# Moving 23 on-chip swaps to ScalarE's DMA queue, some evacuations and roundings to VectorE, in a new order of all instructions

## The chip, the cores and the metric
The kernel runs on one core of one Trainium2 chip. The metric is device time in microseconds from launch to end. The core has TensorE (PE; its weight loads are the row PEld), VectorE (DVE), ScalarE (ACT), GpSimd (POOL) and SyncE (SP), which here only issues DMAs. "q" behind an engine's name is its sequencer, which waits and issues.

## The reference
Two layers (DEPTH 2) over 256 tokens of width 1024, all in float32. Each layer:

```python
n = rmsnorm(h, norm_g[i])
z = n @ w_in[i] + b_in[i]
(c_val, c_glu, c_gate, p_in, p_gate, q, k, v, a_gate, qi, ki, wi) = jnp.split(z, cut, axis=-1)
ya = conv_module(c_val, c_glu, ...) * jax.nn.silu(c_gate)      # depthwise conv of 31 taps, layernorm, 256x256
yb = pool_mixer(p_in, ...) * jax.nn.silu(p_gate)               # causal means over 2, 4, 8, 16 tokens
q, k, qi, ki = rope(q), rope(k), rope(qi), rope(ki)            # rotary: x1*cos - x2*sin, x2*cos + x1*sin
yc = sparse_attention(q, k, v, qi, ki, wi) * jax.nn.silu(a_gate)
h = h + jnp.concatenate([ya, yb, yc], axis=-1) @ w_out[i]
h = h + (p[i] @ ple_w[i]) * jax.nn.sigmoid(h @ ple_gate_w[i])
```

The attention has 8 heads of 64. An indexer (4 heads of 64) scores all keys of a query, the 64 best causal keys take part in the softmax, the others don't. A final rmsnorm closes the trunk.

## The kernel before, in words
Activations lie transposed: 128 features per partition block, 256 tokens along the row. A float32 product is made from three products of rounded parts: each operand is split into `hi` (rounded to TensorE's float32r form) and `lo` (the remainder, also in that form), and hi*hi, hi*lo and lo*hi are summed in a PSUM bank (`mm3`). One such 128x128 block against 256 tokens is three matmuls of 256 columns (line 208, tile `bank`), and the program bundles six of them.

Weights come as chunks of 2048 columns (1024 KB) into a ring of three `raw` tiles by one DMA each on SP's queue (line 294, `dma`). Each chunk has two halves of 1024 columns. A half is rounded to `hi` by a copy (line 242 on ScalarE, 244 on VectorE), and `lo` is raw minus hi (`sub_hi`, line 262 on VectorE, 264 on POOL). `hi` and `lo` have rings of six tiles. A new load has to wait until both halves of the chunk that lay in its `raw` tile have been split.

The input projection is worked chunk by chunk (`gemm_in`, 8 bundles each). Chunk numbers are in the tags: 5 and 6 are Q0 and Q1 (the two halves of q), 7 and 8 are K0 and K1, 9 and 10 are V0 and V1, 13 is QI (the indexer's queries), 3 the pooling input, 2, 4, 11, 12 gates. After a chunk VectorE multiplies the bank with the token's rms factor (line 252, `bank<-bank,rb`), and `evac` adds the bias on ScalarE (line 217).

For a rotary chunk (`rope_pair`) the two evacuations write `z`. Since the rotation mixes partitions 32 apart, four SBUF-to-SBUF DMAs of 64 KB copy quarters of `z` to `zs` with the halves swapped; these are "the swaps". For the indexer key (`e ki`) there are ten of 32 or 64 KB. With five rotary chunks (Q0, Q1, K0, K1, QI) of four swaps and one of ten, a layer has 30 swaps, the kernel 60, all on SP's queue. Then `rope` makes dst = z*cos, zs = zs*sin and dst = dst+zs (lines 252 on VectorE, 254 on POOL); dst is `zrq` for q, `zrk` for k, `qir` for the indexer. `z` and `zs` are rings of two tiles, so a chunk's evacuation waits for the rotation of the chunk two before it.

In the trace the rows `zrk<-z,f` and `zrq<-z,f` are cosine products, `zs<-zs,f` sine products, `zrk<-zrk,zs` and `zrq<-zrq,zs` the adds.

Layer 0's order after that: the indexer scores (4 matmuls each for two blocks of queries, then a relu on ScalarE and weighted sums `sc` on VectorE), the search for the 64 best (8 rounds of MAX8 and MATCH_REPLACE8 on VectorE, lines 651 and 653) which ends in the penalty `pen` (line 275), then attention logits (qk), whose first use on VectorE (line 693, `lg<-bank,pen`) adds the penalty, the exponentials (line 217), transposes (line 212) and the product with v. In between VectorE works through 62 taps of the convolution (line 269, `bank<-f,f,bank`).

What engine does what, and in which order, is not left to a scheduler: `Order.add` collects 1726 operations, each with its possible "ways" (an engine with a cost estimate), and `Order.issue` emits them in the order of the string `ORDER`, two characters for each operation. The number they encode is 3 * operation + way. `PORT` adds a few more waits between operations by number. Within an engine the instructions run in the order in which they are emitted; an instruction that waits holds all behind it on its engine.

```python
i, way = divmod(len(DIGITS) * DIGITS.index(ORDER[2 * k]) + DIGITS.index(ORDER[2 * k + 1]), 3)
assert i not in made and all(d in made for d in self.ops[i][1])
made[i] = self.ops[i][0][way][4]()
```

The end of the kernel (`last_gate`) works with tokens on partitions: gate product, sigmoid, residual, sums of squares, the final scaling and five output DMAs, of which two were already on ScalarE's queue.

Of the kernel before, what the change touches and what calls it, by code (L numbers as in the profile page):

```python
# [87 lines left out]
    "Q3M-TNM1S7KaTQN<S=Q6TTN?Q9TLMgTWNBQ<NEM?Q?MBMEMHN&QBMKN-MNQEN3MjS@V<N9MQQHNHMTMmMpSBMsNKMvSvSEMyQKSISyNNSKTZUQ"
    "QNSONTNWS|NQU$T^NdNgNjNZT#NmNpMWMZS:M^NsMaMdN^T&U+NvNbTaNyQQV?TdQTM|N|O#QWVCSQV|QZSTOHQ^OKO&O*U-O.VEU0QdUUQaON"
    "OQTgOTOWO0OZO3O6O9O<O?OBOEQgQjQmQpU3QsTjU6QvS^QySZU9Q|O^TmW#R#U<TpR&U?TsW(R*R0TvUBR-T*UEVaT-UHR3R6UKR9R<VQVHR?"  # L90
    "VKRBRET0V#XERHUWV&RKRNU[RQVTT3VNRTVyV*VdT6V^VgV-T9VjWaW*VvT<VmW6W.W9U^UaUdZ<UgUjWdUmWhUpUsW0UvWEW3UyWNU|WHV0WB"
    "V3WQV6W^WKWjV9VWVZVpWmXHWZVsWpXNXLZdW<WsYWX*W?WvZ?X&XBWTZBWWX-WyXQX0X3XTX?[0W|X6X#XaZgXWX9Y#ZEZjXyXZX|ZHX<X^Xd"
    "Y*Xg[EXmY-XpY&ZmY0XsXvYEXjZqYHZKY3ZWYNY<ZNY?ZTY6YZ[3Y^YyY9YaY|ZQYKYBYd[HZ#ZZZvYQ[K[9Z^[&Yg[6Zs[<ZaZy[NZ|[Q[*[#"
    "YT[m[?[B[TZ&[W[p[ZZ*[s[^Z-[v[a]?[y[d]B[|]E]#[-[j[g]&]^]*]H]-]0]a]K]dZ0]N]gZ3]jZ6YjYmZ9Yp]mYsYv]p]9]|]Q^#]v]<^&"
    "]T]4^*]X]6]Z^-]s^0^3]y^9^6^<^?^C^N^I^E^Q^K"
# [3 lines left out]
    61: 129, 153: 323, 176: 157, 635: 267, 869: 937, 926: 922, 986: 1027, 987: 988, 992: 878, 1112: 1156,  # L99
    1130: 1129, 1488: 1500, 1684: 1682,  # L100
# [11 lines left out]
class Order:  # L112
# [200 lines left out]
def trunk(ctx: ExitStack, tc: tile.TileContext, xT, pT, w_in, w_ki, w_v, w_out, w_gate, w_ple,  # L313
# [54 lines left out]
    def chunk(tag, src, width=2048, pieces=1, late=VECTOR_LATE):  # L368
# [7 lines left out]
        for a in range(0, width, width // 2):  # L376
# [108 lines left out]
    def layer(l, sqs, ple):  # L485
# [7 lines left out]
        for k in range(0, KT, 2):  # L493
# [4 lines left out]
            R.copy(nhi[:, k:k + 2, :], n, "act dve" if l == 0 else "act")  # L498
# [33 lines left out]
        def evac(dst, pb, c, func):  # L532
            for j in range(2):
                R.act(dst[j], pb[:, j * S:(j + 1) * S], func, bias=bias(c, j))
# [72 lines left out]
        R.act(z[:, 0, :], pt[:, :S], AF.Identity, bias=col(l, SP_B + 28))  # L607
# [23 lines left out]
        for t in (1, 0):  # L631
# [8 lines left out]
            for e in range(2):  # L640
                R.act(pbs[e][:, :2 * nk], pbs[e][:, :2 * nk], AF.Relu, scale=0.125)
# [30 lines left out]
        for t in (1, 0):  # L672
# [3 lines left out]
            for g0 in range(0, 4, nh):  # L676
# [27 lines left out]
                for i in range(nh):  # L704
# [10 lines left out]
                   rinv[:, t, :].rearrange("p (e f) -> p f e", e=2).unsqueeze(3).to_broadcast([128, 4, 2, 64]), "act")  # L715
# [3 lines left out]
            R.copy(wide, on, "act")  # L719
# [31 lines left out]
        for t in range(2):  # L751
            R.act(cn[:, t, :], pc[:, t * 256:(t + 1) * 256], AF.Identity, bias=nm[:, t:t + 1], scale=rl[:, t:t + 1])
# [13 lines left out]
        for j in range(2):  # L766
            R.act(pwb[:, j, :], pw_[:, j * S:(j + 1) * S], AF.Identity, bias=col(l, SP_PWB + j))
# [273 lines left out]
```

## Time and profile before

| what | us |
|---|---|
| median of 3 runs | 340.71 (338.14 to 340.8) |
| the profiled execution, its own time | 336.73 |
| its span, first to last instruction | 334.9 |
| PE busy | 316.4 |
| DVE busy | 243.9 |
| ACT busy | 192.3 |
| POOL busy | 160.7 |

The profiled execution is a single one, 1.2% below the median of the timed runs. Busy times count instructions on the engine's data path, not its waits or DMA issues; matmuls overlap, so that each lasts about 0.28 us in the rows while they start about 0.118 us apart. A row of a timeline is: start, length, engine, line, operation, out<-in, shapes, count, and in brackets how long the engine stood idle before it and what ended that.

### The profile page before, as it was taken

Reading aid. Unit: us, or ns where it says so; the run is one execution under the profiler, and the core shown is the slowest. Engines: PE = TensorE matmul, PEld = TensorE weight load, DVE = VectorE, ACT = ScalarE, POOL = GpSimd, SP = SyncE. Lnnn points to the kernel's source line nnn. Section 1 sums busy time; section 2 is a strip of 40 time slices with the busy share of each in tenths; the row PEclk is TensorE's granted clock in tenths of the full one; section 3 lists DMA queues with packets and bytes.
Section 4 is the critical chain, followed back from the end, with each engine's and each line's share of the span. In section 5 each row is a group of like instructions: output and inputs, shape, how many; then the busy total and the mean of one; then the engine's idle time right before and its main releaser. Section 6 shows DMA issues by size and latency. Waiting matters only on the chain.

```text
span 334.9 us, 6450 instructions
## 1 busy us (share of the span) xinstructions
PE 316.4 (94%) x2468; PEld 295.6 (88%) x2469; DVE 243.9 (73%) x549; ACT 192.3 (57%) x337; POOL 160.7 (48%) x112
## 2 busy tenths in 40 slices
PE   7899999895999999999999999999999999999990
PEld 3789999894889999999999999999888999998870
DVE  3977999895798553758798587998895862558374
ACT  3668434614768863547498544545657583637452
POOL 1004566958986583000112464997978665302011
PEclk9999999997999999999999999999999999999996
DMA  7988675382060309364616747536433327262003
GB/s 211 342 288 324 218 281 191 96 243 95 12 250 2 127 22 387 126 252 137 242 32 238 293 157 278 183 103 240 150 127 125 127 93 283 99 227 119 0 1 126
DMA packets 13551, 57.32 MB, mean 171 GB/s; under 512 B 2128, under 2 KB 3280, under 8 KB 8016
## 3 DMA queue, kind: packets, MB, share of 16 engines
q1 hardware_dynamic: 13232, 56.52, 48.2%
q8 instruction: 19, 0.31, 0.4%
q10 hardware_dynamic: 288, 0.39, 0.3%
q14 instruction: 12, 0.10, 0.1%
HBM read 52.45 MB, written 1.05 MB: 160 GB/s over the span
## 4 chain that ended last, share of the span: by engine, by line
PE 76%; DMA 8%; POOL 4%; SPq 4%; issue 3%; ACT 2%; DVE 1%; POOLq 0%; DVEq 0%
PE bank L208 73%; DMA raw<-in_w_in_dram 5%; SPq L294 4%; DMA zs<-z 4%; PE bank L212 3%; POOL zs L254 1%; POOL qir L254 1%; ACT hi L242 1%; POOL zrk L254 1%; POOL ag L254 0%; POOL zrq L254 0%; DVE zrk L252 0%; POOL acc L254 0%; ACT vt L242 0%; ACT bank L217 0%
## 5 line engine op out<-in xcount | busy, mean ns | idle before, releaser
L208 PE MATMUL bank<-xhi,hi 128*128 128x256 f32 x464 | 133.0, 289 | 0.2 <-ACT ple L242 0.2
L242 ACT ACTIVATE hi<-raw 128x1024 fp32r<-128x1024 f32 (+2 forms) x95 | 94.5, 1015 | 64.8 <-DMA raw<-in_w_in_dram 25.7
L208 PE MATMUL bank<-xlo,hi 128*128 128x256 f32 (+1 forms) x464 | 130.3, 282 | 0.9 <-DVE xlo L262 0.9
L208 PE MATMUL bank<-xhi,lo 128*128 128x256 f32 x448 | 126.3, 282 | 0.3 <-POOL lo L264 0.3
L264 POOL TENSOR_TENSOR lo<-raw,hi 128x1024 fp32r<-128x1024 f32 (+2 forms) x43 | 102.6, 2398 | 46.9 <-ACT hi L242 46.8
L208 PEld LDWEIGHTS bank<-xhi,hi 128*128 128x128 f32 x464 | 87.8, 190 | 2.4 <-issue 1.0
L208 PEld LDWEIGHTS bank<-xlo,hi 128*128 128x128 f32 (+1 forms) x464 | 87.2, 188 | 1.7 <-DVE xlo L262 1.4
L208 PEld LDWEIGHTS bank<-xhi,lo 128*128 128x128 f32 x448 | 85.1, 190 | 0.5 <-POOL lo L264 0.5
L262 DVE TENSOR_TENSOR lo<-raw,hi 128x1024 fp32r<-128x1024 f32 (+2 forms) x55 | 60.1, 1122 | 16.8 <-ACT hi L242 12.9
L269 DVE SCALAR_TENSOR_TENSOR bank<-f,f,bank 128x256 f32<-128x256 f32 x116 | 56.1, 483 | 1.6
L208 PE MATMUL bank<-yhi,hi 128*128 128x256 f32 x128 | 36.6, 286 | 0.0
L208 PE MATMUL bank<-ylo,hi 128*128 128x256 f32 x128 | 36.0, 281 | 0.0
L208 PE MATMUL bank<-yhi,lo 128*128 128x256 f32 x128 | 35.9, 281 | 0.0
L208 PE MATMUL bank<-hi,xhi 128*128 128x256 f32 (+2 forms) x100 | 32.1, 321 | 0.8 <-DVE vt L252 0.8
L208 PE MATMUL bank<-lo,xhi 128*128 128x256 f32 (+2 forms) x100 | 31.3, 313 | 0.0
L208 PE MATMUL bank<-hi,xlo 128*128 128x256 f32 (+2 forms) x100 | 31.2, 312 | 0.0
L252 DVE TENSOR_TENSOR bank<-bank,rb 128x512 f32<-128x512 f32 (+1 forms) x26 | 17.2, 674 | 15.0 <-PE bank L208 14.8
L208 PEld LDWEIGHTS bank<-ylo,hi 128*128 128x128 f32 x128 | 24.1, 188 | 0.3 <-DVE ylo L262 0.3
L208 PEld LDWEIGHTS bank<-yhi,hi 128*128 128x128 f32 x128 | 24.1, 188 | 0.2
L208 PEld LDWEIGHTS bank<-yhi,lo 128*128 128x128 f32 x128 | 24.1, 188 | 0.0
L208 PEld LDWEIGHTS bank<-hi,xhi 128*128 128x128 f32 x100 | 18.8, 188 | 2.7 <-DVE vt L252 1.0
L208 PEld LDWEIGHTS bank<-hi,xlo 128*128 128x128 f32 x100 | 18.9, 188 | 1.3
(165 smaller groups left out, 457.3 us busy)
## 6 DMA issues: line engine op xcount, KB each, us to landing
raw<-in_w_in_dram SPq DMA_DIRECT2D x25, 1024.0 KB, 5.7
raw<-in_w_out_dram SPq DMA_DIRECT2D x8, 1024.0 KB, 4.9
raw<-in_w_gate_dram SPq DMA_DIRECT2D x8, 1024.0 KB, 5.2
zs<-z SPq DMA_DIRECT2D x40, 64.0 KB, 2.3
raw<-in_w_v_dram SPq DMA_DIRECT2D x2, 1040.0 KB, 5.9
raw<-in_w_ple_dram SPq DMA_DIRECT2D x8, 256.0 KB, 4.6
f<-in_xT_dram SPq DMA_DIRECT2D x4, 256.0 KB, 6.5
raw<-in_w_in_dram SPq DMA_DIRECT2D x4, 256.0 KB, 6.0
```

Source lines behind the costliest of these rows:

```text
L208: lambda: self.nc.tensor.matmul(o, lhsT, rhs, start=start, stop=stop, skip_group_check=True))],
L212: self.add([("pe", 195, 109, None, lambda: self.nc.tensor.transpose(o, i, ident))], [i, ident], [o], sort=2)
L242: ways.append(self.on_act(o, i, lambda: self.nc.scalar.activation(o, i, AF.Copy)))
L252: ways.append(self.on_dve(n, lambda: self.nc.vector.tensor_tensor(o, a, b, op), late=late))
L254: ways.append(self.on_pool(n, lambda: self.nc.gpsimd.tensor_tensor(o, a, b, op)))
L262: ways.append(self.on_dve(n, lambda: self.nc.vector.tensor_tensor(o, a, hb, OP.subtract), late=late))
L264: ways.append(self.on_pool(n, lambda: self.nc.gpsimd.tensor_tensor(o, a, hb, OP.subtract)))
L269: self.add([self.on_dve(o.free_size(), lambda: self.nc.vector.scalar_tensor_tensor(o, a, s, b, op0=op0, op1=op1), len(ptr))], [a, b] + ptr ...
L294: self.add([("dma", nbytes, 590 if inner else 440, None, lambda: q.dma_start(o, i))], [i] if i.space != bass.MemoryType.DRAM else [], [o] ...
```

## The change
Three of the helpers get a second way. `dma` lets an SBUF-to-SBUF transfer be issued from ScalarE; `affine` and `relu8` stand in place of ScalarE activations that only add a bias, scale, or clamp, and can run on VectorE. Several copies that were ScalarE's alone ("act") may now be VectorE's too ("act dve"). `ORDER` and `PORT` are new as a whole.

Read operation by operation, the new string issues 23 of the 60 swaps from ScalarE: two of the indexer key's ten in each layer; two of QI's in each layer; in layer 0 one of Q0's, one of Q1's, three of K0's and one of K1's; in layer 1 two of Q0's, four of Q1's, two of K0's and one of K1's. 31 instructions go from ScalarE to VectorE (seven roundings of a 1024-column weight half, three of 512 columns, five roundings of 512 columns of `xhi`, three of `yhi` and the rest smaller), 12 from VectorE to ScalarE, one from POOL to ScalarE, 19 from POOL to VectorE (eight of them `lo` of a weight half), 17 from VectorE to POOL (three of them `lo` of a weight half). The work itself is the same.

The order on TensorE keeps the sequence of stages. Around layer 0's attention it now has one bundle of K1 (1, not 2) before the scores, and between K0's last bundle and the first logits 7 bundles of K1, 7 of V1, 6 of the pooling input and the scores, where it had 7, 8, 2 and the scores. POOL's order there was, from the scores on: cosine of Q0, sine of Q0, cosine of QI, sine of QI, add of Q0, add of QI, `lo` of V1, cosines of K0 and Q1, two `lo` of the pooling input, sines of K0 and Q1, adds of K0 and Q1. It is now: cosine of Q0, cosine of QI, sine of Q0, sine of QI, add of QI, `lo` of V1, add of Q0, two `lo` of the pooling input, cosines of K0 and Q1, sines of K0 and Q1, adds of K0 and Q1. On SP's queue the load of chunk 4 stands ahead of three swaps of Q1 and one of K0; on ScalarE's the three other swaps of K0 stand behind K0's second evacuation, followed by a relu, a rounding and Q1's swap.

```diff
 ORDER = (
...
 PORT = {
...
+    def affine(self, o, i, bias, scale=None):
+
+        half = PSUM not in (i.space, o.space)
+        ptr = [bias] if scale is None else [scale, bias]
+        kw = {} if scale is None else {"scale": scale}
+        args = (bias, None, OP.add) if scale is None else (scale, bias, OP.mult, OP.add)
+        self.add([self.on_act(o, i, lambda: self.nc.scalar.activation(o, i, AF.Identity, bias=bias, **kw), len(ptr)),
+                  self.on_dve(o.free_size(), lambda: self.nc.vector.tensor_scalar(
+                      o, i, args[0], args[1], op0=args[2], **({} if scale is None else {"op1": OP.add})), len(ptr), half)],
+                 [i] + ptr, [o], True)
+
+    def relu8(self, o):
...
     def dma(self, o, i, nbytes, eng="sp"):
         q = {"sp": self.nc.sync, "act": self.nc.scalar}[eng]
         inner = i.space != bass.MemoryType.DRAM and o.space != bass.MemoryType.DRAM
-        self.add([("dma", nbytes, 590 if inner else 440, None, lambda: q.dma_start(o, i))],
-                 [i] if i.space != bass.MemoryType.DRAM else [], [o] if o.space != bass.MemoryType.DRAM else [])
+        ways = [("dma", nbytes, 590 if inner else 440, None, lambda: q.dma_start(o, i))]
+        if inner:
+            ways.append(("act", 2200, 560, None, lambda: self.nc.scalar.dma_start(o, i)))
+        self.add(ways, [i] if i.space != bass.MemoryType.DRAM else [], [o] if o.space != bass.MemoryType.DRAM else [])
...
-                    split(raw[:, a + c:a + c + q], hi[:, c:c + q], lo[:, c:c + q], "dve pool", late, "act dve" if pieces > 1 else "act")
+                    split(raw[:, a + c:a + c + q], hi[:, c:c + q], lo[:, c:c + q], "dve pool", late, "act dve")
...
-            R.copy(nhi[:, k:k + 2, :], n, "act dve" if l == 0 else "act")
+            R.copy(nhi[:, k:k + 2, :], n, "act dve")
...
-            R.copy(yhi[:, k:k + 2, :], y, "act")
+            R.copy(yhi[:, k:k + 2, :], y, "act dve")
...
-            R.copy(hhi[:, r, :], h[:, r, :], "act")
+            R.copy(hhi[:, r, :], h[:, r, :], "act dve")
...
```

## Rows read from the trace of the kernel before

**Rows 1.** The page's first part: TensorE's busy time, share of the span, instructions.
```profile
PE 316.4 (94%) x2468; PEld 295.6 (88%) x2469; DVE 243.9 (73%) x549; ACT 192.3 (57%) x337; POOL 160.7 (48%) x112
```

**Rows 2.** Stretches: length, busy us by engine, PE's clock, DMA share.
```profile
0.00:30.00 30.00, 25.67 (x173) 21.09 (x175) 20.20 (x39) 17.27 (x26) 3.51 (x13) 1.00 0.86 291
...
75.40:79.40 4.00, 0.38 (x5) 0.18 (x3) 2.72 (x12) 2.94 (x6) 3.79 (x4) 1.00 0.35 145
...
79.40:84.00 4.60, 4.60 (x20) 3.79 (x20) 1.51 (x3) 1.19 (x2) 3.60 (x3) 0.63 0.18 45
...
84.00:88.60 4.60, 4.60 (x39) 4.41 (x38) 4.27 (x21) 3.56 (x7) 4.60 (x3) 1.00 0.08 21
...
84.00:120.00 36.00, 35.98 (x296) 32.15 (x294) 28.42 (x95) 28.17 (x66) 25.90 (x20) 1.00 0.24 91
...
120.00:228.00 108.00, 108.00 (x884) 105.89 (x885) 80.16 (x146) 60.48 (x92) 43.87 (x26) 1.00 0.55 197
...
228.00:241.00 13.00, 12.52 (x102) 11.16 (x100) 11.67 (x42) 8.86 (x17) 10.76 (x8) 1.00 0.58 194
...
325.50:334.90 9.40, 1.59 (x12) 1.40 (x12) 4.55 (x11) 2.98 (x9) 1.94 (x2) 0.70 0.30 112
```

**Rows 3.** Timeline of PE, 59.5 to 84 us.
```profile
61.78 1.67 PE L208 MATMUL bank<-qir 64*128 64x256 f32 x14 [1.22 <-POOL qir L254]
...
79.38 0.70 PE L208 MATMUL bank<-zrk,zrq 64*128 64x256 f32 x2 [3.62 <-POOL zrk L254]
```

**Rows 4.** Timeline of POOL, 50 to 80 us.
```profile
55.47 1.29 POOL L254 TENSOR_TENSOR zs<-zs,f 128x512 f32<-128x512 f32 x1 [2.84 <-DMA zs<-z]
...
60.47 1.26 POOL L254 TENSOR_TENSOR qir<-qir,zs 128x512 f32<-128x512 f32 x1
...
61.69 2.41 POOL L264 TENSOR_TENSOR lo<-raw,hi 128x1024 fp32r<-128x1024 f32 x1
...
66.86 4.79 POOL L264 TENSOR_TENSOR lo<-raw,hi 128x1024 fp32r<-128x1024 f32 x2
...
75.61 2.49 POOL L254 TENSOR_TENSOR zs<-zs,f 128x512 f32<-128x512 f32 x2 [3.96 <-DMA zs<-z]
...
78.06 1.26 POOL L254 TENSOR_TENSOR zrk<-zrk,zs 128x512 f32<-128x512 f32 x1
```

**Rows 5.** Swaps into zs issued 65 to 72 us: issue ns, us to landing.
```profile
L294 SPq DMA_DIRECT2D zs<-z x5: 512/582/1439, 66.6 to 70.2; - x5
...
DMA to landing us min/median/max: 5.4/7.3/7.9
```

**Rows 6.** Timeline of SP's queue around 65 us.
```profile
65.53 1.07 SPq L294 DMA_DIRECT2D raw<-in_w_in_dram  x1
```

**Rows 7.** Timeline of ACT around 74 us.
```profile
74.37 2.01 ACT L242 ACTIVATE hi<-raw 128x1024 fp32r<-128x1024 f32 x2 [7.39 <-DMA raw<-in_w_in_dram]
```

**Rows 8.** The page's DMA issues: KB each, median us to landing.
```profile
raw<-in_w_in_dram SPq DMA_DIRECT2D x25, 1024.0 KB, 5.7
```

**Rows 9.** Timeline of DVE, 63 to 85 us.
```profile
63.56 0.48 DVE L269 SCALAR_TENSOR_TENSOR sc<-bank,wi,f 128x256 f32<-128x256 f32 x1 [1.08 <-ACT bank L217]
...
76.68 0.35 DVE L269 SCALAR_TENSOR_TENSOR sc<-bank,wi,sc 128x128 f32<-128x128 f32 x1 [1.65 <-ACT bank L217]
...
79.49 1.22 DVE L275 TENSOR_SCALAR pen<-sc 128x256 f32<-128x256 f32 x1
...
84.30 0.42 DVE L693 CUSTOM_DVE_ANT_0 lg<-bank,pen 128x256 f32<-128x256 f32 x1 [3.39 <-PE bank L208]
```

**Rows 10.** Timeline of ACT's queue at the end.
```profile
330.96 0.34 ACTq L294 DMA_DIRECT2D out_dram<-ag  x1
```

**Rows 11.** Groups by line and form: count, busy us, mean ns, idle before.
```profile
L242 ACT ACTIVATE hi<-raw 128x1024 fp32r<-128x1024 f32 x82 | 85.0, 1055 | 58.9 <-DMA raw<-in_w_in_dram 25.7 <-PE bank L208 21.6 <-DMA raw<-in_w_gate_dram 6.2
...
L262 DVE TENSOR_TENSOR lo<-raw,hi 128x1024 fp32r<-128x1024 f32 x41 | 49.1, 1230 | 15.1 <-ACT hi L242 11.2 <-PE bank L208 3.8
...
L244 DVE CAST hi<-raw 128x512 fp32r<-128x512 f32 x5 | 2.1, 424 | 1.3 <-DMA raw<-in_w_ple_dram 1.3
```

More of the change, by code (lines that the diff above doesn't have):

```diff
@@ L94 @@
[L94 to L95 removed]
+    "#Z#m###j#&#*#p#-%y#0#K#3#N#6%|#9#d#_#Q#<#b#?#B#s#}$##v&##g$B#y$E#W$($3$*$H&*#T$K&&$6&-$Q%3%7&B$T$W$p%:$9&0(9%<"
+    "$<$N$Z%@%B&Q&3$?$.&W%F&6$0#E#H%W%H$a%K$d&9%N&^%Z%R$g&<%_$j%T$s&d$^&?&j%a)3&E&p$v&v&K&H&|$y&N&T(<$m&Z$|)g&a(?%#"
+    "&g)<*Q%&&m%*)6)?(B(E(H%d)9%g(K&s%j+<)p%m(N(Q%0&y)j)t%p%s(T(W%w)B(Z(&(#(^*Z(d)E(*(m*T)H*^(s)K(a*W)N(|)Q(-)m.^+?"
@@ new lines @@
+    ")T(p(3(0(y)W+C3p(j*a(6+E-s)Z3s*d)^3v*g(h+I3y(w*j)a3|4#*m.a4&*p4*/H*s)$4-40*v.e)v.g*y)y43)d46)|+#)&.j*#*&)*7p49"
+    "+K).*|-v4<**+44?*-4B)14E*04H-z+-+N-|*3+0+Q4K+**94N+T*64Q*<+W.#/K%-+Z*B+(/N+^6g*@+a*F4T*I.&4W4Z.*+7+d.-4^+j+g4a"
+    "*L.0/Q7g4d.34g6j*O.64j4m.m4p/U.94s.<,&.?,*,y+:8N4v,-,0,3+v-#4y,|,6+p,9/W6n.B4|+s6p,<.p5#,?-&.E5&.s.N.L,B6t.R5*"
+    ".v,E.I5-.y--,H7s.|50,K.U9-/#53+n,N/&-*+z/Z/*/^,Q.X/0,T/a7y,W56/d+}8Q,Z6v59,^/-.[/g,a5<6y,d,$-06|,g-37#,j8U/6/:"
+    "-6,m7&90/<5?7*-9/3,p/j,s-<,v/v-?94/y/|/m0&-B0*8^-E0-5B8a-H/@005E-K8d8W/C0#/p030B068g-N0E5H/F090H0<7--Q0?5K70-T"
@@ new lines @@
+    "0K8[-W5N0N0^-Z0Q5Q0T0W0v0Z0|0y961&1#0a0d1*0g:K0j0m5T0p1-239:29-^0s/s2?-a105W8j-d1B13-g16191E1<8m-j1?;05Z8p1H-m"
+    "5^-q731K2E7}262<5a792B2K1v1N5d1Q1T1W8s2N1Z5g9<2Q767w2T1y5j1^2W1a5m1d1g1j1m2Z1p5p2H1s5s2^1|9?7<9^2a2#2&9B7@2s5v"
+    "7B5y5|6#2*7F9E6&2-6*7L9H2v;32y2|7I2d6-2g2j3#2m8#607OA?63203&8&662p8v9K3*7R3-9N7U3W699Q6=7X308y3336398*:N3=8-9T"
+    "3Z6B6?9b3?3B9W3E3H3K:Q3N3Q3T3^3a3d3g6E6H7Z3j6K806N3m836Q8|7^9d:T7a6T6W:W6Z6^7d<T7m867k9Z9#6a89:39&9m8<9g9p9*8?"
+    ":69s;99j:p9v8B6e;p:a8E:d:y8I9y8K9|:::#:&:Z:*:m:^:<:-;-:0;<:|;y:s:v;*;6;s:g:j;#:?=g;&:B;K;|;?:E;Q<^;T;E:H;N<W;v"
@@ new lines @@
+    ";B;W;Z<a;j>K;d;g;H<Z;^=j<#<&?0<6;m<0;a<3=q<N<H=s<*<<<-=n<9<B<?<d<K<Q<E?K<g>T<j<|=#>N<m=3=9<p=-==<s=@<v?3<y=&=B"
+    "=0=6>Q=E=*=v?9=|=K=IAK>#=y=^=N>&>0?=>->*>3?N>?>9><AB?Q>a>d>6>B>W>H>g>Z?6AN>j>E?#=TC#>y=Q>|AH>^=bAQAE>s?&=X?U?g"
+    "?j=d?mSW=Z>v?W>p>m??AZ?pAa?B?sAe?E?v?y?|AU?H@aA^?Z?^@dAX?a?d@g@#@T@&D*@j@*@WC3@-BH@0@Z@3BF@6B9@_@9?-B=@p?*@m@H"
+    "AgB@@<@s@?C&Ak@K@vAvC-AmBRBBAyBTC*BKApBW@BC0A|@ND-@Q@EC6D0E#B#AsCBC9C<B&BNB-A-B*A0CHA#C?@yCNA&EWCEA3FBA*BaCK@|"
+    "B_CQA6BZCTBeA9CWBgB0A<CZE&CaE-E*CgB3CmE0EaBjBmEZC^BpHyBsCdE^CjEdD3BvByCpB|D6IdCvD9D<D?CsCyDBDED#DHFEE3DKDOE6C|"
@@ L100 @@
-    1130: 1129, 1488: 1500, 1684: 1682,
+    84: 159, 176: 157, 192: 300, 295: 294, 599: 294, 635: 267, 774: 775, 887: 889, 893: 909, 926: 992, 1027: 1135,
+    1029: 1028, 1050: 1110, 1107: 1106, 1418: 1415, 1424: 1422, 1453: 1415, 1488: 1500, 1603: 1665, 1606: 1658,
+    1672: 1682, 1684: 1682, 1697: 1685,
 }
@@ L219, in act @@
                  [i] + ptr, [o] + ([] if accum is None else [accum]))
+    def affine(self, o, i, bias, scale=None):
[8 more added lines that the diff above has]
+    def relu8(self, o):
+        self.add([self.on_act(o, o, lambda: self.nc.scalar.activation(o, o, AF.Relu, scale=0.125)),
+                  self.on_dve(o.free_size(), lambda: self.nc.vector.tensor_scalar(o, o, 0.125, 0.0, op0=OP.mult, op1=OP.max))],
+                 [o], [o])
     def on_act(self, o, i, issue, ptr=0, table=None, accum=False):
@@ L533, in evac @@
             for j in range(2):
-                R.act(dst[j], pb[:, j * S:(j + 1) * S], func, bias=bias(c, j))
+                if func == AF.Identity:
+                    R.affine(dst[j], pb[:, j * S:(j + 1) * S], bias(c, j))
+                else:
+                    R.act(dst[j], pb[:, j * S:(j + 1) * S], func, bias=bias(c, j))
         def rope(z, zs, dst):
```

59 lines of the change are left out of this document (21 added, 38 removed).

## The prediction, made before the changed kernel was run

> **What bounds the kernel now.** I first read the busy shares. TensorE is busy 316.4 us of the 334.9 us span [rows 1], so the end is set by TensorE's own work plus the places where it stands still. The table by stretches says where those are [rows 2]: between 84 and 120 us and between 120 and 228 us it is busy all the time (35.98 of 36.00, 108.00 of 108.00), from 228 to 241 us it loses 0.48 us, in the first 30 us 4.33 us, in the last 9.4 us 7.81 us. The one large hole in the middle is from 75.4 to 79.4 us: 0.38 of 4.00 us. The stretch after it costs as well: its granted clock is 0.63, most of it thus at the lower level (1.2 GHz), and 20 matmuls run in 4.6 us, against 39 in the 4.6 us behind it at clock 1.00. Nineteen matmuls at 4.6/39 = 0.118 us are 2.2 us lost.
>
> The TensorE timeline names both waits of that region [rows 3]: 1.22 us before the indexer scores (for the rotated `qir`, from POOL), and 3.62 us before layer 0's first attention logits (for `zrk`, from POOL). I then followed the second back. POOL's timeline [rows 4]: POOL stood idle for 3.96 us until swaps of `z` into `zs` had landed, and could start the two sine products only at 75.61; the add that writes `zrk` came at 78.06. The swaps were issued between 66.6 and 70.2 us and took 5.4 to 7.9 us to land [rows 5]. Ahead of them in the same queue stood a 1024 KB weight load, issued at 65.53 [rows 6], whose first reader, a rounding on ScalarE that had stood waiting for 7.39 us, started at 74.37 [rows 7]: a landing time of 8.8 us, where the median of such loads is 5.7 us [rows 8]. So the chain is: load, swaps behind it in SP's queue, POOL's three rotation steps, TensorE.
>
> **The change part by part, against the profiled execution (336.73 us, span 334.9; the median of the runs shown, 340.71, is 1.2% above it).** A bundle is six 256-column matmuls, 6 x 0.118 = 0.71 us [rows 2].
>
> *Scores of layer 0.* In the new order the cosine product of `qir` stands ahead of the products that wait for swaps and the add into `zrq` behind it, so one product goes into the 2.84 us in which POOL waited [rows 4] and one add goes behind: the last add of `qir` ends about 1.24 + 1.26 = 2.5 us earlier than 61.73, at 59.2. TensorE stands before the scores one bundle earlier, at 60.56 - 0.71 = 59.85 (60.56 is 61.78 less 1.22). The wait of 1.22 us goes. Of the eight swaps that gate it three now go out from ScalarE.
>
> *First logits of layer 0.* POOL's list from that point to the `zrk` add is now: one `lo` (2.41), the `zrq` add (1.30), two `lo` (4.79), two cosine products (2.6), two sine products (2.49), the `zrk` add (1.26), together 14.85 us [rows 4], so 59.2 + 14.9 = 74.1. TensorE comes there with three bundles more in front (20 bundles between K0's last matmul and the first logits, 17 before), at 75.76 - 1.22 + 2.1 = 76.7, or 76.1 if the head gains what I give it below. The margin is about 2 us. Swaps: three of K0's four go out from ScalarE behind its second evacuation of K0; the fourth, and three of Q1's four, stand on SP behind the same weight load. That load waits for the `lo` now ending at 61.6, and lands at 67 (5.7 us) or 70.4 (8.8 us); the swaps behind it by 68 to 71.3. POOL wants them 3.7 us before its add is done, at 70.4. At the worse end the add ends at 75, still ahead of TensorE. So 3.62 us go, and with them the stretch at the lower clock, 2.2 us: it came behind that standstill.
>
> *What is late next.* The logits' first use needs the top-64 penalty, which VectorE finishes at 79.49 + 1.22 us [rows 9]. Its chain began at 63.56, idled 1.65 us for ScalarE (which was held by the weight load), and afterwards VectorE waited 3.39 us for the logits. Started 2.5 us earlier and without the idle time it ends at about 76.5, when the first logits are done. Then VectorE has no slack left there. From 84 to 120 us it is busy 28.42 of 36.00 us, ScalarE 28.17, POOL 25.90 [rows 2], and TensorE will ask for their results some 7 us earlier. I give back 1.5 us for this (0 to 5).
>
> *Issuing on ScalarE.* 23 issues at the 0.58 us of SP's rows [rows 5] are 13.3 us; the one SBUF-to-HBM issue of ScalarE shown took 0.34 us [rows 10], so 7.8 to 13.3 us. Against that 31 instructions go from ScalarE to VectorE and 13 come (12 of them from VectorE): seven weight roundings at 1.055 [rows 11] and 24 smaller ones of 512 columns or fewer, estimated at half of that, are some 20 us out, some 7 in. ScalarE's sum stays as it is. VectorE gains the seven weight roundings at twice 0.424 for twice the columns (6 us), eight `lo` at 1.23 and some 30 smaller ones, and loses three `lo` and some 26 smaller ones: about +14 us [rows 11], in stretches such as 120 to 228 us, where it is busy 80.16 of 108.00 us. TensorE's buffers hide that; if they don't, each `lo` that comes late costs up to its 1.23 us. I take 1.0 us for new waits there (0 to 4). A swap at the head of ScalarE's queue holds what stands behind it: behind K0's three these are the last score relu, a weight rounding, a swap of Q1, then K1's evacuation.
>
> *Head, layer 1, tail.* The first loads are reordered within the same bytes; TensorE idles 4.33 us there at a DMA share of 0.86 [rows 2]. I take 0.6 us gain (0.9 gain to 1 us loss). In layer 1 two bundles more stand before the first logits, and 0.48 us of idle time can go: 0.4. The scores of layer 1 get one bundle less of cover; I set that off against the swaps of QI that no longer stand behind a load. In the tail one scaling goes from VectorE to ScalarE ahead of another there: 0, within 0.4.
>
> Sum: -1.2 - 3.6 - 2.2 - 0.6 - 0.4 + 1.5 + 1.0 = -5.5, with some 0.4 us more of short restarts behind each wait: -5.9 us, 330.8 against 336.73, a ratio of 0.9825. On the median of 340.71 that is 334.8 us.
>
> *One rule weighed.* In all rows swaps and loads share SP's queue, and the swaps land with the load [rows 5 to 7]; no run here shows two queues at once. The Trainium skill (DMA: Bandwidth & Descriptors, "Issuing engines are not separate DMA queues") says that transfers started by different engines run on the same 16 DMA engines and interleave, so that several issuers save only issue time. By that rule alone K0's three swaps land no earlier than the load, 67 to 70.4 us. The sum above uses only that bound for them and would stay; what the rule takes away is spare time, and it is the ground for the first rival.
>
> **The rivals.**
> Rival 1, K0's wait stays in part. The load ahead of the swaps goes out as late as before (65.5), because its buffer's last `lo` is late or earlier waits on SP hold it, and takes 8.8 us. For: four of the eight swaps of this pair still stand on SP behind it; SP's order is in place. Against: POOL's list frees the buffer four microseconds earlier. Then sine products start at 74.6, `zrk` is done at 78.4, TensorE waits about 2 us and the slow stretch stays: of the 5.8 us only 1.6 to 2 are gained, and the total is -1.9: 334.8 on this execution, 338.8 on the median.
> Rival 2, the gain is handed back. TensorE arrives 7 us earlier at attention and the gates, and VectorE with 14 us more becomes the bound between 84 and 130 us. For: 28.42 of 36.00 us busy already. Against: 4.9 us of its idle time here was waiting for TensorE and for ScalarE's hold. With 5 us handed back (the end of that bound): -2.4, or 338.3 on the median.
> Rival 3, slower: ScalarE's queue is held by swaps. Each swap waits in order for the rotation before it in the same `zs` buffer; a rotation late on POOL holds ScalarE, and with it score relus and weight roundings. The row of the 7.39 us hold [rows 7] shows such a hold, then on data. If holds of that size come in both layers where roundings are not ahead, TensorE stands still 4 us and runs one stretch at 1.2 GHz each time, 2 x (3.6 + 2.2) = 11.6, less the 5.9: +5.7, 346.4 on the median. It decides from holds of about 5 us in each layer on; below that the roundings are ahead, as the 7.39 us did not themselves stop TensorE. Against: the new order puts the roundings for the next bundles ahead of the swaps.
>
> **How the numbers follow.** A run of this kernel can be told from no change at about 1%, 3.4 us. Forecast 0.67 (own range 331 to 337), rival 1 0.14, rival 2 0.12, rival 3 0.07. The first counts as faster (0.67), the two middle ones as the same (0.26), the last as slower (0.07). The range 331.0 to 341.0 takes in the forecast with the low end of the give-back and both middle rivals.
>
> **What would show it.** Right: no TensorE wait over 1 us between 55 and 90 us and granted clock 1.00 throughout; POOL without waits for `zs` over 1 us; K0's ScalarE swaps landing in about 3 us. Wrong: a wait for `zrk` of 2 us or more (rival 1); TensorE waits for VectorE's `lg` or `lo` between 84 and 130 us (rival 2); ScalarE rows with swaps that waited 5 us and a later TensorE wait for `hi` (rival 3).

## The result, and the profile after

| what | before | after |
|---|---|---|
| median of 20 runs, us | 337.85 (334.58 to 341.3) | 333.36 (331.71 to 335.11) |
| ratio | | 0.9882, interval 0.9858 to 0.9907 |
| the profiled execution, us | 336.73 | 334.27 |
| its span | 334.9 | 332.2 |

The change makes the kernel 1.2% faster by the ratio, 4.5 us (1.3%) by the medians. The first three runs of before had given 340.71; with 20 the median is 337.85. The ratios leave out runs more than 1.5% above the fastest of their kernel; since the runs of before spread over more than 2%, that keeps their faster part, and so below the ratio of the medians of all runs stands beside each.

The profiled pair is only 2.46 us apart: before ran 1.1 us under its median, after 0.9 us over. What follows compares places in the two traces, not sums.

The busy times of the page (compare [rows 1]):

```profile
PE 315.4 (95%) x2468; PEld 294.1 (89%) x2469; DVE 255.0 (77%) x570; ACT 181.2 (55%) x319; POOL 154.0 (46%) x109
```

VectorE has 11 us more than its 243.9, ScalarE 11 less than 192.3, POOL 7 less than 160.7. ScalarE's DMA issues don't count as busy.

The same stretches as in [rows 2] (length, busy us of PE, PEld, DVE, ACT, POOL, PE's clock, DMA share, GB/s):

```profile
75.40:79.40 4.00, 3.94 (x29) 3.22 (x28) 3.97 (x19) 2.37 (x4) 4.00 (x4) 1.00 0.02 6
79.40:84.00 4.60, 3.44 (x24) 2.97 (x25) 2.14 (x13) 4.28 (x9) 4.60 (x3) 1.00 0.24 59
84.00:120.00 36.00, 35.83 (x299) 32.72 (x298) 29.22 (x89) 24.51 (x59) 18.78 (x17) 1.00 0.36 127
228.00:241.00 13.00, 12.35 (x100) 11.07 (x100) 11.06 (x48) 10.68 (x23) 12.80 (x8) 1.00 0.33 103
```

The hole from 75.4 to 79.4 us is filled (0.38 before, 3.94 now), and the stretch behind it runs at clock 1.00 where it had 0.63. From 84 to 120 us TensorE is busy 35.83 of 36.00 us with VectorE at 29.22 (35.98 and 28.42 before); from 228 to 241 it loses 0.65 us, before 0.48. What TensorE still waits for is in its timeline (compare [rows 3]):

```profile
60.60 1.57 PE L209 MATMUL bank<-qir 64*128 64x256 f32 x14 [1.16 <-POOL qir L272]
...
80.56 0.39 PE L209 MATMUL bank<-xhi,lo 128*128 128x256 f32 x1 [1.22 <-POOL lo L282]
...
203.80 1.13 PE L209 MATMUL bank<-qir 64*128 64x256 f32 x8 [1.08 <-ACT z L228]
...
268.35 0.33 PE L213 MATMUL bank<-f,c 128*128 128x128 f32 x1 [0.71 <-ACT c L228]
...
268.93 0.55 PE L213 MATMUL bank<-f,c 128*128 128x128 f32 x3 [0.25 <-DVE c L229]
```

The wait for K0's `zrk` is gone. The wait before layer 0's scores is as long as it was (1.22, now 1.16). Four waits are new: 1.22 us for a `lo` on POOL right behind the first logits, 1.08 us before layer 1's scores, and 0.71 and 0.25 us at layer 1's normalization of the convolution. One more grew, for a `zrk` before layer 1's logits, from 0.29 to 0.60 us.

To see where time is won and given back I lined up the two traces by the work that TensorE has done (each matmul at the usual spacing of its form) and read when each has reached the same amount:

```
work done, us    before    after    after - before
 50               55.93    55.50    -0.43
 65               72.95    72.27    -0.68
 70               84.41    77.40    -7.01
 75               89.35    84.84    -4.51
160              176.89   172.10    -4.79
200              217.52   213.50    -4.02
250              270.35   266.29    -4.05
260              281.62   279.18    -2.44
300              321.69   319.16    -2.54
```

7.0 us stand gained once layer 0's first logits are through. 2.5 go again within the next 5 us of work, nothing between 84 and 180 us, 0.8 at layer 1's scores, and 1.6 at its normalization. Of the 2.5 us 1.4 come with the wait for the `lo`; most of the rest is the wider spacing of the logits' matmuls, which the kernel before has ahead of the mark of 70 us, so that the 7.0 flatter the gain. The table compares two executions, and two of the same order can differ by nearly 2 us in it: e1 below, which has the changed kernel's order in layer 0, stands 2.9 us ahead of before at 75 us of work, not 4.5.

POOL's timeline around the first of these places (compare [rows 4]):

```profile
54.10 2.14 POOL L272 TENSOR_TENSOR qir<-z,f 128x512 f32<-128x512 f32 x1 [1.39 <-DMA zs<-z]
...
57.91 1.30 POOL L272 TENSOR_TENSOR zs<-zs,f 128x512 f32<-128x512 f32 x1 [0.42 <-DMA zs<-z]
...
59.29 1.26 POOL L272 TENSOR_TENSOR qir<-qir,zs 128x512 f32<-128x512 f32 x1
...
74.35 1.30 POOL L272 TENSOR_TENSOR zs<-zs,f 128x512 f32<-128x512 f32 x1 [1.68 <-issue]
...
75.61 1.30 POOL L272 TENSOR_TENSOR zrk<-zrk,zs 128x512 f32<-128x512 f32 x1
...
78.09 4.77 POOL L282 TENSOR_TENSOR lo<-raw,hi 128x1024 fp32r<-128x1024 f32 x2
```

QI's cosine (54.10) took 2.14 us, where such products take 1.29, and POOL had waited 1.39 us ahead of it; the add of `qir` (59.29) ended at 60.55, not at 59.2 as forecast. The sine of Q1, which POOL's order has ahead of the `zrk` add (75.61), came at 74.35, 1.7 us behind the sine of K0, and so the `lo` that TensorE needed at 79.3 was done only at 80.5.

The swaps of Q1 and K0, with the load ahead of them (issue in ns and time, then us from issue to landing). First SP's, the load's landing in the first line; then the three of K0 that ScalarE issued:

```profile
DMA to landing us min/median/max: 5.4/5.4/5.4
...
L312 SPq DMA_DIRECT2D zs<-z x4: 507/547/582, 63.4 to 65.9; - x4
...
DMA to landing us min/median/max: 4.6/5.5/6.2
```

```profile
L314 ACTq DMA_DIRECT2D zs<-z x3: 515/612/848, 65.9 to 67.3; - x3
...
DMA to landing us min/median/max: 3.7/4.4/4.8
```

Compare [rows 5]. The load was issued at 62.9, not 65.53, and landed in 5.4 us, not 8.7, at 68.4; these seven swaps landed between 68.7 and 71.0, those of ScalarE behind those of SP. They were in time because the load was early, not because they passed it. Q1's fourth swap, which ScalarE issued at 68.70, landed only at 74.2, behind the load that SP issued at 68.95 (74.0).

### The profile page after: what moved, and what is told of

It reads as the page before. It is cut to its first block, busy times and chain, and to the rows that moved or that the text cites. A ratio compares the mean times of both kernels' runs of the same rounds, so it can differ in the third digit from the quotient of the medians.

```text
span 332.2 us, 6467 instructions
## 1 busy us (share of the span) xinstructions
PE 315.4 (95%) x2468; PEld 294.1 (89%) x2469; DVE 255.0 (77%) x570; ACT 181.2 (55%) x319; POOL 154.0 (46%) x109
## 3 DMA queue, kind: packets, MB, share of 16 engines
HBM read 52.45 MB, written 1.05 MB: 161 GB/s over the span
## 5 line engine op out<-in xcount | busy, mean ns | idle before, releaser
L282 POOL TENSOR_TENSOR lo<-raw,hi 128x1024 fp32r<-128x1024 f32 (+1 forms) x40 | 93.6, 2351 | 70.4 <-DVE hi L262 40.1
L260 ACT ACTIVATE hi<-raw 128x1024 fp32r<-128x1024 f32 (+2 forms) x89 | 87.3, 1007 | 54.1 <-PE bank L209 24.4
L280 DVE TENSOR_TENSOR lo<-raw,hi 128x1024 fp32r<-128x1024 f32 (+2 forms) x58 | 64.9, 1147 | 9.5 <-ACT hi L260 9.2
L228 ACT ACTIVATE z<-bank,f 128x256 f32<-128x256 f32 x21 | 9.3, 470 | 20.6 <-DMA zs<-z 9.2
```

The lines of the kernel that those rows point to most:

```text
L228: self.add([self.on_act(o, i, lambda: self.nc.scalar.activation(o, i, AF.Identity, bias=bias, **kw), len(ptr)), self.on_dve(o.free_size(), ...
L260: ways.append(self.on_act(o, i, lambda: self.nc.scalar.activation(o, i, AF.Copy)))
L280: ways.append(self.on_dve(n, lambda: self.nc.vector.tensor_tensor(o, a, hb, OP.subtract), late=late))
L282: ways.append(self.on_pool(n, lambda: self.nc.gpsimd.tensor_tensor(o, a, hb, OP.subtract)))
```

## The experiments

Operations are named by their numbers; A is the new order, B that of before, a pair is (operation, way). The runs come in three groups, each beside its own runs of before, whose medians are 336.19 us for e, 338.54 for f and 337.06 for h. Differences under 1 us between groups are not resolved.

**e1 and e2: the two halves of the order.** The orders have cuts at which the same operations but one are out; the one used lies at the end of layer 0's output projection. The waits in `PORT` go with their operations.

```diff
-ORDER = A
+ORDER = A[:770] + [x for x in B if x not in A[:770]]      # e1
+ORDER = B[:770] + [x for x in A if x not in B[:770]]      # e2
```

> The new order up to the last bundles of layer 0's output projection (770 operations), the order of before from there on. Theory: layer 0 carries the whole gain and layer 1 gives part of it back (the two traces stand 4.9 us apart at the end of layer 0 and 2.5 us at the end), so this is 1.5 to 2.5 us faster than the changed kernel, a ratio of about 0.981 to before. Rival (what layer 1 seemed to lose belongs to that one execution): as the changed kernel, 0.986 to 0.991.

> The reverse: the order of before in layer 0, the new one from the end of layer 0's output projection on. Theory: slower than before by 1.5 to 2.5 us (ratio 1.005 to 1.008), with TensorE waits of about 1 us before layer 1's scores. Rival: within 0.3% of before.

e1: 331.88 us, ratio 0.9867 (0.9809 to 0.9926), 0.987 by the medians. That is the changed kernel's ratio: layer 0 holds the gain, as the theory had it, but layer 1's loss of 1.5 to 2.5 us did not show in the time. e2: 340.91 us, ratio 1.0115 (1.0065 to 1.0165), slower than the theory had it. Its trace loses 1.1 us against before from 160 us of work on (145.87 against 144.80 up to 300); the other 3 us lie ahead of the cut, where its order is that of before, and partly close to the seam (1.02 us for a `lo` at 159 us). Part of them is the clock: behind its `zrk` wait of 3.48 us it is 0.51 over 6.9 us, from 79.0 to 85.9, where before has 0.63 over 4.6 us [rows 2]. So e2 says that the new second half brings no gain, not what it costs.

**e3: all swaps on SP again.**

```diff
-(swap, 1)  # ScalarE, 23 swaps
+(swap, 0)  # SP, same places in A
```

> The changed kernel with all 23 swaps issued from SP again, nothing else moved. Theory (the new order, not the issuing engine, removes the wait): within 1.5 us of the changed kernel. Rival (ScalarE's queue takes K0's swaps past the weight load): the TensorE wait for zrk comes back with 2 to 4 us and the stretch at the lower clock behind it, 3 to 6 us slower than the changed kernel.

341.77 us, ratio 1.0167 (1.0114 to 1.022), 9.9 us above e1 in the same group, against the theory. But the rival's place was wrong too: no wait for `zrk` came back in layer 0. TensorE's timeline has it before the scores, and behind it comes a stretch at the lower clock:

```profile
66.75 2.92 PE L205 MATMUL bank<-qir 64*128 64x256 f32 x14 [6.33 <-POOL qir L268]
```

```profile
63.50:70.30 6.80, 3.56 (x17) 3.14 (x18) 1.42 (x5) 3.75 (x7) 6.14 (x5) 0.50 0.13 18
```

SP's queue shows why: two of QI's swaps stand right behind the load of chunk 3, and land in 6.8 to 7.1 us.

```profile
56.00 0.52 SPq L308 DMA_DIRECT2D raw<-in_w_in_dram  x1
...
56.55 1.14 SPq L308 DMA_DIRECT2D zs<-z  x2
```

```profile
L308 SPq DMA_DIRECT2D zs<-z x2: 507/548/590, 56.6 to 57.1; - x2
...
DMA to landing us min/median/max: 6.8/6.9/7.1
```

In the changed kernel ScalarE issued those two at 52.5 and 53.2, ahead of that load, and they landed in 2.0 to 2.1 us. By the line-up 4.9 of the 8.9 us between the traces of e3 and e1 are there at 160 us of work; the rest comes in layer 1, where the two also differ in order.

**f0 to f3: which transfers must stand ahead of which load.** f0 is the changed kernel, as a yardstick.

```diff
-..., 562, 189, 191, ...    # f1: e3's order; 562 loads chunk 3, 189 and 191 are QI's swaps
+..., 189, 191, 562, ...
-..., 614, 235, 314, 315, 312, 237, ...    # f2: B; 614 loads chunk 4, the rest are swaps of Q1 and K0
+..., 235, 314, 315, 312, 237, 614, ...
-(313, 1), (315, 1), (312, 1)    # f3: A; K0's three swaps
+(313, 0), (315, 0), (312, 0)
```

> The changed kernel as it is, beside the others on one chip. Both theories: 0.984 to 0.992 of before. If the stretches in which the runs of its two halves differed from it are chance, this execution shows a TensorE wait before layer 0's scores of another size than 1.2 us, between 1 and 3.

> All 23 swaps on SP, and one weight load (chunk 3) moved behind QI's two swaps that stood behind it in that version. Theory (what ScalarE's queue gives is a place ahead of a waiting load, not a faster transfer): the 6.5 us wait before layer 0's scores falls to 1 to 3 us and the time to within 3 us of the changed kernel. Rival (a second queue by itself lands the swaps sooner): the wait stays above 4 us and the time is 5 us or more above the changed kernel.

> The kernel before, with one weight load (chunk 4) moved behind the five swaps of Q1 and K0 that stood behind it on SP. Theory (this load holds K0's swaps): the 3.6 us TensorE wait for zrk falls under 1.5 us and the stretch at the lower clock goes, 3 to 5 us faster than before. Rival (the load, now later, holds ScalarE and VectorE's penalty in its place): the wait moves to the logits or to hi, and the time is within 1.5 us of before.

> The changed kernel with K0's three swaps on SP again, the other 20 on ScalarE. Theory (the prediction's own bound: in the new order they land in time behind the load too): no wait for zrk over 1 us, within 1 us of the changed kernel. Rival (K0's swaps need ScalarE's queue): a wait for zrk of 2 to 4 us and the lower clock behind it, 3 to 6 us slower.

f0: 333.60 us, 0.985 of before by the medians, but a ratio of 0.998 (0.9933 to 1.0027), which alone would show no gain; its waits are those of the changed kernel, 1.23 us before the scores and 1.25 for the `lo`.

f1: 337.94 us (ratio 1.0046, 1.0004 to 1.0089). With the load behind them QI's swaps land in 2.2 to 3.2 us, and the wait is 2.07 us, not 6.33:

```profile
L308 SPq DMA_DIRECT2D zs<-z x3: 588/589/589, 55.3 to 56.5; - x3
...
DMA to landing us min/median/max: 2.2/2.7/3.2
```

```profile
62.49 2.30 PE L205 MATMUL bank<-qir 64*128 64x256 f32 x14 [2.07 <-POOL qir L268]
```

The wait did as the theory said, the time stayed 4.3 us above f0, outside the 3 us allowed. Behind the wait the clock is 0.51 from 63.1 to 66.6 us. By the line-up of its trace with f0's 0.9 us of the 4.3 are there at 160 us of work, and 3.4 us come in layer 1, where 13 more swaps are back on SP (its scores wait 1.21 us, those of f0 not at all).

f2: 333.57 us, the same as f0, with one operation moved in the order of before (ratio 0.9947, 0.9898 to 0.9997; 0.985 by the medians). The five swaps, and POOL behind them:

```profile
L308 SPq DMA_DIRECT2D zs<-z x5: 588/590/1396, 66.0 to 69.4; - x5
...
DMA to landing us min/median/max: 2.0/2.0/3.2
```

```profile
67.38 4.80 POOL L278 TENSOR_TENSOR lo<-raw,hi 128x1024 fp32r<-128x1024 f32 x2
...
72.13 2.54 POOL L268 TENSOR_TENSOR zs<-zs,f 128x512 f32<-128x512 f32 x2
...
74.63 1.28 POOL L268 TENSOR_TENSOR zrk<-zrk,zs 128x512 f32<-128x512 f32 x1
```

They land in 2.0 to 3.2 us where [rows 5] has 5.4 to 7.9, and POOL's sines follow its `lo` with no idle time. TensorE starts the first logits (76.21) without a wait, and the clock behind them is 1.00. But a later wait, for K1's `zrk`, brings a stretch at the lower clock back:

```profile
76.21 0.70 PE L205 MATMUL bank<-zrk,zrq 64*128 64x256 f32 x2
...
87.20 1.13 PE L205 MATMUL bank<-zrk,zrq 64*128 64x256 f32 x4 [1.31 <-POOL zrk L268]
```

```profile
79.40:84.00 4.60, 4.60 (x39) 4.49 (x39) 4.60 (x23) 4.14 (x8) 3.20 (x3) 1.00 0.20 51
...
89.50:93.00 3.50, 3.50 (x23) 2.52 (x21) 3.40 (x16) 1.99 (x8) 2.84 (x3) 0.51 0.68 220
```

So of 5.2 us gained at 75 us of work 2.3 are left at 80. Perhaps not every run does this: the profiled one (335.26 us) is one of five of 335.2 to 336.7 us, with mean clocks of 0.984 to 0.989, and the other seven, 332.3 to 333.6 us, have 0.990 or more. The load is issued at 70.1 and lands in 4.8 us, 0.6 us later than with the load in front ([rows 7]):

```profile
74.93 2.01 ACT L256 ACTIVATE hi<-raw 128x1024 fp32r<-128x1024 f32 x2 [7.42 <-DMA raw<-in_w_in_dram]
```

The theory holds; of the rival only this is left, that some of the wait moves.

f3: 332.27 us (ratio 0.9883, 0.9843 to 0.9923; 0.9815 by the medians), 1.3 us below f0, a little more than the theory's 1 us. In layer 0 there is no wait for `zrk`, and none for the `lo`:

```profile
72.77 2.54 POOL L268 TENSOR_TENSOR zs<-zs,f 128x512 f32<-128x512 f32 x2
...
75.28 1.28 POOL L268 TENSOR_TENSOR zrk<-zrk,zs 128x512 f32<-128x512 f32 x1
...
77.77 2.38 POOL L278 TENSOR_TENSOR lo<-raw,hi 128x1024 fp32r<-128x1024 f32 x1
```

Both sines run without a gap. In the changed kernel ScalarE first issued K0's three swaps and only then Q1's:

```profile
65.88 2.04 ACTq L314 DMA_DIRECT2D zs<-z  x3
...
67.97 0.37 ACT L235 ACTIVATE bank<-bank 128x256 f32<-128x256 f32 x1 [2.18 <-issue]
...
68.70 0.79 ACTq L314 DMA_DIRECT2D zs<-z  x1
```

2.18 us of ScalarE's idle time is its own issuing, and Q1's swap went out at 68.70, together with the next load (its issue lasted until 69.49, the load's from 68.95 to 69.28), and took 5.5 us. In f3 it went out at 67.2, 3.7 us ahead of that load, and took 4.2.

**e4 and h4: the 31 instructions back on ScalarE**, in the changed kernel and in f3.

```diff
-(copy or bias, 1)  # VectorE, 31 operations
+(copy or bias, 0)  # ScalarE
```

> The changed kernel with the 31 instructions that went from ScalarE to VectorE back on ScalarE, in the same places of the order. Theory (VectorE's gain of work is hidden and so is ScalarE's loss of it): within 1 us of the changed kernel. Rival (the moves are what gives ScalarE room for the swaps): 1.5 to 4 us slower, with TensorE waits for hi. Rival on the other side (VectorE's extra work holds the lo parts): 1 to 2 us faster.

> The changed kernel with K0's three swaps on SP and the 31 instructions back on ScalarE. Theory (undoing the 31 moves alone cost 3 us because K0's swaps on ScalarE came late by a hair, a TensorE wait of 2 us for zrk): with those on SP no wait for zrk, and within 1 us of the version with K0's swaps on SP, 0.979 to 0.985 of before by the medians. Rival (the moves relieve ScalarE everywhere): 2 us or more slower than that version, 0.988 or above.

e4: 334.75 us, ratio 0.9938 (0.9896 to 0.9981), 0.996 by the medians. h4: 332.61 us, ratio 0.9925 (0.9884 to 0.9965), 0.987 by the medians. Undoing the moves costs some 3 us in the changed kernel (2.9 above e1) and 1.8 us with K0's swaps on SP (0.987 against f3's 0.9815, in different groups). In e4's profiled execution (336.23 us, 1.5 above its median) the wait for K0's `zrk` is back:

```profile
78.99 1.44 PE L205 MATMUL bank<-zrk,zrq 64*128 64x256 f32 x5 [1.81 <-POOL zrk L268]
```

The clock behind it is 0.66 from 79.0 to 84.0 us. ScalarE issued the last of K0's swaps at 69.46 and Q1's at 70.17, behind a load that SP had issued at 69.18, and they landed at 75.0 and 75.3. h4's trace has no such wait, but its time lies between what the theory and the rival gave. So the moves help, in one execution of e4 visibly through ScalarE's room for the swaps; what they give besides was not settled.

**h1 and h2: a version that beats both.** h1 takes f3 up to the cut and before's order behind it; h2 also makes two edits ahead of layer 0's scores.

```diff
-ORDER = A
+ORDER = f3[:770] + [x for x in B if x not in f3[:770]]    # h1
-..., 63, 190, 562, 189, 191, ...    # h2: 63 is the small mats load
+..., 190, 562, 189, 191, 63, ...
-PORT 192: 300    # QI's cosine on POOL waited for a lo on VectorE
```

> The new order in layer 0 with K0's three swaps on SP, and the order of before from the end of layer 0's output projection on. Theory (K0's swaps on ScalarE cost 1.3 us in layer 0, the new layer 1 costs some 1.2 us against the old one, 146.0 against 144.8 us over the same stretch of TensorE's work): 2 to 3 us faster than the changed kernel, 0.977 to 0.981 of before by the medians. Rival (the two don't add): as the version with K0's swaps on SP alone, 0.982.

> The same, with two edits ahead of layer 0's scores: the small mats load, which stood on SP ahead of one of QI's swaps, behind them, and without the added wait that holds QI's cosine on POOL for a lo on VectorE. Theory (QI's rotation sets the 1.2 us wait before the scores): that wait falls to 0.8 us or less, 0.3 to 0.8 us faster than without the two edits. Rival (the swaps' landing sets it, and that doesn't move): the same wait and time.

h1: 330.36 us, ratio 0.9845 (0.9794 to 0.9896), 0.980 by the medians: the fastest of all, by 2% or 6.7 us against before. Against f3 (0.9815) the old layer 1 gives 0.5 us, less than the theory's 1.2 and not resolved between two groups. The waits of 0.71 and 0.25 us at layer 1's normalization are in none of the versions with the old order of layer 1.

h2: 331.89 us (ratio 0.9886, 0.9848 to 0.9923), 1.5 us slower than h1; the theory falls. QI's last swap landed 1.9 us earlier than in the changed kernel, and POOL's cosine no longer waited, but VectorE's two `lo` beside it and the sines took 4.52 us:

```profile
52.75 4.52 DVE L276 TENSOR_TENSOR lo<-raw,hi 128x1024 fp32r<-128x1024 f32 x2
```

```profile
52.68 1.28 POOL L268 TENSOR_TENSOR qir<-z,f 128x512 f32<-128x512 f32 x1
...
54.79 3.63 POOL L268 TENSOR_TENSOR zs<-zs,f 128x512 f32<-128x512 f32 x2 [0.83 <-DMA zs<-z]
...
58.50 1.28 POOL L268 TENSOR_TENSOR qir<-qir,zs 128x512 f32<-128x512 f32 x1
```

In the changed kernel the same two took half of that:

```profile
52.74 2.35 DVE L280 TENSOR_TENSOR lo<-raw,hi 128x1024 fp32r<-128x1024 f32 x2
```

What stood behind them on VectorE came later, and TensorE's scores, whose wait was again 1.15 us, were now released by VectorE:

```profile
60.34 0.99 PE L205 MATMUL bank<-qir 64*128 64x256 f32 x7 [1.15 <-DVE psb L266]
```

The wait that I took away had kept POOL's cosine off the first of the two `lo`. The two edits were not run apart, so how much of the 1.5 us each costs is not shown.

**h3: only the issuer.**

```diff
-(swap, 0)  # B, 23 swaps on SP
+(swap, 1)  # ScalarE, same places in B
```

> The order and the engines of before, with only the issuing of the 23 swaps moved to ScalarE, each at its old place in the order. Theory (K0's swaps then no longer stand behind the load on SP, but three of Q1's four stay on SP behind nothing new): the zrk wait of 3.6 us shrinks to 0 to 2 us, ScalarE's roundings come later where swaps wait at the head of its queue; 1 to 4 us faster than before. Rival (without the new order ScalarE's queue is held by swaps whose data is late): waits for hi on TensorE, 1 to 5 us slower than before.

335.28 us, ratio 0.9963 (0.9915 to 1.0012), 0.995 by the medians: 1.8 us faster, hardly resolved, at the low end of the theory. The `zrk` wait is 1.05 us. But of K0's swaps only one overtook the load, by 1.3 us. The load was issued at 62.78 and landed at 70.8; the first line is its landing, then ScalarE's three swaps, which landed at 69.5, 71.0 and 71.5:

```profile
DMA to landing us min/median/max: 8.0/8.0/8.0
...
L310 ACTq DMA_DIRECT2D zs<-z x3: 514/516/651, 63.0 to 64.2; - x3
...
DMA to landing us min/median/max: 6.5/7.3/7.4
```

6.5 to 7.4 us, as on SP ([rows 5]: 5.4 to 7.9). What came earlier is the load: SP, with fewer swaps to issue, sent it 2.7 us before the time in [rows 6] (1.7 us of that this whole trace is ahead at that place), and the swaps with it.

## Why the prediction was right, and where it was not

The time, the direction and the range were right; the size was 4.5 us by the medians for a forecast of 5.9. That 334.8 came within 1.4 us of the median is in part luck. It set out from a median of three runs that 20 runs put 2.9 us lower, and the terms were worked out against the profiled execution, whose pair is only 2.5 us apart. By the line-up that pair has about 0.7 us of gain at the head (0.6 forecast), none at layer 0's scores (1.2), 5.2 at the first logits (5.8), then 1.4 of loss at the `lo` and 2.3 in layer 1. The last 0.4 us of the sum, for restarts, rested on no row, and no run here measures them.

**Right: the first logits, -3.6 and -2.2.** The diagnosis (load, swaps behind it, POOL, TensorE) is shown by f2, in which one moved operation takes away the wait for K0's `zrk` and the lower clock right behind it. The -2.2 was a little large: a clock of 0.63 over 4.60 us [rows 2] is 1.7 us short of full speed, and the rest of the missing matmuls is the wider spacing of the logits, which remains. The load went out at 62.9, 1.3 us later than I had it, and landed at 68.4, within my bounds of 67 to 70.4; seven of the eight swaps had landed by 71.0, where I had 71.3 at the latest. Q1's fourth, from ScalarE, came at 74.2, outside my bound, and with it `zrk` was done at 76.9 where I had 74.1 to 75, just as TensorE arrived: the margin of 2 us was used up. It held in f0 and e1 too, but not in e4's execution, where `zrk` came 1.81 us late. Of the signs only the clock came as I had it (1.00 from 55 to 90 us): TensorE waited 1.16 and 1.22 us there, and POOL 1.39 and 1.68 us.

**Right: the rule that was weighed.** The Trainium skill (DMA: Bandwidth & Descriptors, "Issuing engines are not separate DMA queues") has transfers of several issuers interleave on the same engines. The traces agree: in the changed kernel and in h3 the swaps from ScalarE landed with the load that SP had issued before them, between 1.3 us ahead of it (one, in h3) and 2.6 us behind. That they land no earlier than the load does not follow from interleaving, and the one in h3 did. My list of signs broke that rule: it asked for K0's swaps to land in about 3 us, and they took 3.7 to 4.8.

**Wrong: scores of layer 0, -1.2.** The step "one product goes into the 2.84 us in which POOL waited" counted POOL's order alone. The new order has, in `PORT`, a wait of QI's cosine for a `lo` on VectorE (1.39 us; the row names a swap that landed at about the same time, but e1's row names the `lo`, and in h2, without the entry, the wait is gone). The cosine then took 2.14 us beside VectorE's second `lo`, and POOL waited 0.42 us for the last swap. The step gave 0.

**Wrong place: the give-back of 1.5 us at 84 to 120 us by VectorE.** That stretch lost nothing. The penalty came at 78.3 us, not 76.5, and VectorE was busy 3.97 of the 4.00 us from 75.4 on, but TensorE did not wait for it. The loss of that kind, 1.22 us, came at 79.3 to 80.5 us, on POOL, through ScalarE's issuing of K0's swaps ahead of Q1's (f3 removes it). I had seen that K0's swaps hold a swap of Q1 in ScalarE's queue, and gave it no price.

**Wrong sign: layer 1, -0.4.** "I set that off" was an offset without a number, and its ground was wrong: QI's swaps do stand behind a load there. SP issued it at 193.4, and it landed at 200.1. The four swaps, two from each queue, went out from 195.2 on and landed at 200.3 to 200.9; VectorE's sine waited for them:

```profile
193.43 0.38 SPq L312 DMA_DIRECT2D raw<-in_w_in_dram  x1
```

```profile
L314 ACTq DMA_DIRECT2D zs<-z x2: 522/690/859, 195.2 to 195.8; - x2
...
DMA to landing us min/median/max: 5.1/5.2/5.3
```

```profile
201.13 0.69 DVE L270 TENSOR_TENSOR zs<-zs,f 128x512 f32<-128x512 f32 x1 [2.72 <-DMA zs<-z]
```

The next bank on VectorE, the `z` on ScalarE and with it TensorE's scores came late in turn. The scores there wait 1.08 us in the profiled execution (0 to 1.58 in the other versions with this order; in f0 VectorE waited 1.43 us and TensorE not at all), and the normalization 0.96. Its 0.7 us are in every version with the new order of layer 1, also with the 31 instructions back on ScalarE (e4, h4), so they belong to the order and not to VectorE's added work. The +1.0 that I took for new waits and the 0.4 of gain together stand against about 2 us of loss in the profiled pair.

**Issuing on ScalarE.** An issue took 0.51 to 0.87 us, median 0.58, together 14.3 us, a little over the upper end of my bounds. VectorE gained 11 us, forecast 14, and TensorE has no wait over 0.2 us between 84 and 180 us.

**The rivals.** Rival 1 did not come in the changed kernel; rival 2 had the handing back right in kind, not the engine. Rival 3, holds of ScalarE, was there in the small (4.5 us of ScalarE's waiting for swaps at 74 us) and stopped TensorE in layer 0 only by the 1.2 us told above. What I did not see is that in this order the swaps from ScalarE are needed: on SP two of QI's stand behind the load of chunk 3, and e3, with this and its layer 1, loses some 10 us.

## What to carry to other kernels

Read which transfers stand in front of a small, urgent one, on all issuing engines together and in order of issue: here a second issuing engine carried it past a large load already under way in one case only, by 1.3 us, but it can send it before a load for which the first engine's queue waits. Try the single move that the chain of waits points to before a new order of everything: here one load moved behind five swaps gave as much as the whole change. An issue on ScalarE cost it 0.58 us (median), and everything behind it in its queue the same. And read each term of a forecast against the traces: a time that comes out right can be a sum of terms that did not.

## What I had not expected of the hardware

Swaps of 64 KB landed in 2.0 us with no load ahead (f2) and, close behind one of 1 MB, in 3.7 to 7.9 us (the changed kernel and [rows 5]). POOL's products and VectorE's subtractions of two SBUF tiles cost each other time: in h2 two `lo` took 4.52 us beside POOL's cosine and sines, and the two sines 3.63 us; in the changed kernel the two `lo` took 2.35 us, and the cosine, begun while the second ran, 2.14 us, where it takes 1.28 in h2. The Trainium skill (SBUF — State Buffer, "Who interferes with whom") has the two engines share a pair of ports as an exclusive lock; these rows agree with it.

And the same order differs in its waits from one execution to the next: layer 0's scores waited 1.16 us in one trace of the changed kernel, 2.49 us in e1 and not at all in h1, which have the same order up to there. The times of before go with the granted clock: of its 87 runs beside the experiments 12 have a mean clock of 0.99 or more and a median of 334.4 us, the other 75 a median of 337.9 us; of the 20 runs of the changed kernel 19 lie at 0.991 or more. This fits a gain that comes in good part from stretches at the lower clock that stay away; that each of the 75 has the wait for K0's `zrk` is not shown, since one run was profiled.
